# A decoder trunk's sparse layer: compressed scores right behind their keys, a new split of two weaves, and the last output tile in two pieces

## The chip, the cores and the metric

The kernel runs on one core of a Trainium2 chip. The core has five engines, each with its own stream of instructions: TensorE (PE; its weight loads are the row PEld), VectorE (DVE), ScalarE (ACT), GpSimd (POOL) and SyncE (SP), and 16 DMA engines. The metric is the time of one execution on the device in microseconds (us), of the whole program.

## What is computed

Two decoder layers over 256 tokens of width 1024, everything in f32. Layer 0 mixes with two sparse attentions side by side (MoBA and NSA, 8 heads each), layer 1 with differential attention; each is followed by a SwiGLU block of width 2816. Each sub-layer is normed, shifted and scaled by rows that come from a conditioning vector `c`, and its result is gated by such a row.

```python
def reference(x, c, ...):
    for i in range(DEPTH):
        mod = jax.nn.silu(c) @ ada_w[i] + ada_b[i]
        sh_a, sc_a, g_a, sh_f, sc_f, g_f = jnp.split(mod[:, None, :], 6, axis=-1)
        h = rms_norm(x, attn_norm[i]) * (1.0 + sc_a) + sh_a
        y = sparse_mixer(h, ...) if i % 2 == 0 else diff_mixer(h, ...)
        x = x + g_a * y
        h = rms_norm(x, ffn_norm[i]) * (1.0 + sc_f) + sh_f
        x = x + g_f * swiglu(h, ffn_w_gate[i], ffn_w_up[i], ffn_w_down[i])
    return x
```

The change lies in NSA's part of layer 0 and in the last lines of layer 1. NSA adds three attentions per head, each with its gate: over compressed keys and values, over selected blocks, over a window. With 256 tokens the last two cover all earlier tokens, each with its own keys. The compressed branch makes 15 keys and 15 values per group out of overlapping stretches of 32 tokens:

```python
def nsa_compress(t, pos_emb, w1, w2):
    blocks = t[:, :, idx] + pos_emb
    hid = jax.nn.silu(jnp.einsum('bgnld,lde->bgne', blocks, w1))
    return jnp.einsum('bgne,ed->bgnd', hid, w2)
...
        p_c = masked_softmax(jnp.einsum('bgrqd,bgnd->bgrqn', qg, kc) * scale, ok_c)
        o_c = jnp.einsum('bgrqn,bgnd->bgrqd', p_c.astype(vc.dtype), vc)
```

## The kernel before

**Precision and weights.** A large matmul is made of three (`mm3`, L250): both operands are split in a high and a low half, and high by high, high by low and low by high are added up in PSUM. `wunit` (L235) brings in one unit of weights: a load of 512 KB into one of five buffers `raw` (issued on SP, L240), then ScalarE writes the high half (`hi`, L188) and VectorE the low one (`lo`, L189). A `raw` buffer comes free with VectorE's half. The compression's weights (L1072) go through the same five `raw` buffers, but TensorE reads them there, so they come free with its matmuls. Loads of conditioning weights by `ada` (L276) have two buffers of their own (`araw`); those of `ada_pe` (L329) use `raw`.

**Order.** The program is written as generators, each of which yields after a piece of work. `weave` (L46) takes turns among several by weight: the generator whose count of turns divided by its weight is lowest goes next. The framework's scheduler then sets each engine's order out of that program and of its own estimates, so a change in the text at one place moves instructions on all engines nearby.

**Layer 0's sparse part.** A first weave (L1298) runs three generators. The first is `nsa_phase` (L975), followed by part of `nsa_heads` (L1152), weight 22; the second is `moba_proj` (L1175), the q, k and v projections of MoBA, weight 20; the third is `ada(0, 2)`, conditioning, weight 9. `nsa_phase` finishes NSA's queries and keys, then compresses keys (turn `v` = 0 of its loop) and values (`v` = 1): 16 products with the weights `w1` into a bank of the group CB (L1072 to L1076), a silu, a small product. For the keys the result is written to `kcT` (L1095). Only after both turns come the compressed scores (`kcT` by `qT` into a bank of CB), their softmax in `scc` (L1126 to L1140: VectorE, with one exp on ScalarE, L1133), two transposes on TensorE (L1144) and a copy to `pcT` (L1146). `nsa_heads` makes eight softmax steps, two for each pair of heads (two maps each, `softmax_maps` L878: scores, exp, then normalise and three transposes per map, L911, copied to `pT`, L913). After the second step of a pair it adds the compressed part (`vblk` by `pcT`). It yields three times per pair, and `first(nh, 6)` (L1280) lets six of its twelve turns run in the first weave: the four steps of the first two pairs.

A second weave (L1305) runs what is left of `nsa_heads`, then `moba_heads` (four steps), weight 22, against two `ada_pe` (conditioning products on TensorE, `raw` by `cs`), weight 14. Then comes the output projection. PSUM's eight banks are dealt out by group in `banks` (L89): in the first weave CB is bank 3 and TR (transposes) banks 6 and 7.

**The end.** The last SwiGLU block keeps its last three pairs of down-projection rows for two passes, one per half `t` of the tokens, each in two halves `f` of 512 columns (L679). `res_norm` (L442) then does, per half: multiply the bank by the gate row (L452), add to the residual (L455) and, at the very end, send it out (L457).

Of the kernel before, what the change touches and what calls it, by code (L numbers as in the profile page):

```python
# [17 lines left out]
P = 128  # L18
S = 256
# [45 lines left out]
def tile_trunk(ctx: ExitStack, tc: tile.TileContext, x, c, positions, ada_w, ada_b, attn_norm, ffn_norm,  # L65
# [36 lines left out]
    def tmp(shape, tag, bufs, dt=F32):  # L102
        return sp.tile(shape, dt, name=nm(tag), tag=tag, bufs=bufs)
# [338 lines left out]
    def res_norm(t, bs, g, i, js, hts):  # L442
# [117 lines left out]
    def ffn(i, hts, nxt, before_tail):  # L560
# [112 lines left out]
        for t in range(NT):  # L673
            keep = chain[:]
            chain[:] = tail
            for fs in ((0,), (1,)):
                for k in ks:
                    down_mm(t, k, us[k - ks[0]], fs)
            tail[:] = chain  # L679
            chain[:] = keep  # L680
            res_norm(t, BS, rows[(i, 5)], *nxt)
            yield
# [292 lines left out]
    def nsa_phase(hts):  # L975
# [72 lines left out]
        G.memset(kcT, 0.0)  # L1048
        vblk = tmp([P, 8, 64], "vblk", 1)
        for v in range(2):  # L1050
# [38 lines left out]
            if v == 0:  # L1089
# [26 lines left out]

        sc = tmp([P, NT, 4, 2, 16], "scc", 1)
        b = bank(*CB)
        for t in range(NT):
            for pr in range(4):  # L1120
                o = (t * 4 + pr) * 32
                mm(b[:, o:o + 32], lhsT=qT[:, pr, t * P:(t + 1) * P],
                   rhs=kcT[:, pr // 2].rearrange("p h n -> p (h n)"), start=True, stop=True)
        for t in range(NT):
            st = sc[:, t].rearrange("p a b n -> p (a b) n")
            V.tensor_tensor(out=st, in0=b[:, t * P:(t + 1) * P].rearrange("p (h n) -> p h n", n=16),  # L1126
                            in1=maskm[:, t:t + 1, :].broadcast_to([P, 8, 16]), op=ALU.add)
            V.tensor_tensor(out=st, in0=st, in1=nrs[:, t, :].unsqueeze(2).broadcast_to([P, 8, 16]), op=ALU.mult)
        s16 = sc.rearrange("p t a b n -> p (t a b) n")
        mx = tmp([P, 16], "cmx", 1)  # L1130
        V.tensor_reduce(out=mx, in_=s16, axis=AX.X, op=ALU.min)
        V.tensor_tensor(out=s16, in0=s16, in1=mx.unsqueeze(2).broadcast_to([P, 16, 16]), op=ALU.subtract)
        A.activation(out=s16, in_=s16, func=AF.Exp, scale=-1.0)  # L1133
        sm = tmp([P, 16], "csm", 1)
        V.tensor_reduce(out=sm, in_=s16, axis=AX.X, op=ALU.add)
        V.reciprocal(out=sm, in_=sm)
        V.tensor_tensor(out=sm.rearrange("p (t h) -> p t h", t=NT), in0=sm.rearrange("p (t h) -> p t h", t=NT),
                        in1=gts[:, :, 0:8], op=ALU.mult)
        V.tensor_tensor(out=s16, in0=s16, in1=sm.unsqueeze(2).broadcast_to([P, 16, 16]), op=ALU.mult)
        V.tensor_tensor(out=s16[:, 0:8, :], in0=s16[:, 0:8, :],  # L1140
                        in1=valid0.unsqueeze(1).broadcast_to([P, 8, 16]), op=ALU.mult)
        b = bank(*TR)
        for t in range(NT):
            T.transpose(out=b[:, t * P:(t + 1) * P], in_=sc[:, t].rearrange("p a b n -> p (a b n)"), identity=ident)  # L1144
        pcT = tmp([P, S], "pcT", 1)
        A.activation(out=pcT, in_=b[:, 0:S], func=AF.Copy)  # L1146
        yield
# [138 lines left out]
    def late(*gens):  # L1286
        for g in gens:
            yield from g
# [9 lines left out]
    weave((late(np_, first(nh, 6)), 22), (moba_proj(hts), 20), (ada(0, 2, pin=True), 9))  # L1298
# [6 lines left out]
    weave((late(nh, moba_heads(*om)), 22), (late(*[ada_pe(0, j, bank_tiles[3]) for j in (4, 3)]), 14))  # L1305
# [58 lines left out]
```

## Time and profile before

| | |
|---|---|
| time, median of three runs | 751.43 us (750.35 to 752.98) |
| the profiled execution | 752.87 us, of which the profile's span is 750.8 |
| mean granted clock of TensorE in it | 0.984 |
| PE, share of the span | 94% |
| DVE, ACT, POOL | 67%, 55%, 5% |
| DMA, bytes and mean rate | 159.41 MB, 212 GB/s |

The span is one execution as the profiler saw it; a row of a timeline gives the start in us from the span's start, the time from first start to last end of the records in it, the engine, the line, out<-in with the program's names, the shape, and how many records (x). In square brackets stands the idle time of that engine just before, and what ended it. Matmuls overlap, so the spacing of starts is what one costs. A matmul of plain f32 operands shows as two records, one of split halves as one. In rows of windows the granted clock of TensorE (PEclk) is a share of 2.4 GHz; 0.50 is 1.2 GHz.

### The profile page before, as it was taken

Reading aid. Unit: us, or ns where it says so; the run is one execution under the profiler, and the core shown is the slowest. Engines: PE = TensorE matmul, PEld = TensorE weight load, DVE = VectorE, ACT = ScalarE, POOL = GpSimd, SP = SyncE. Lnnn points to the kernel's source line nnn. Section 1 sums busy time; section 2 is a strip of 40 time slices with the busy share of each in tenths; the row PEclk is TensorE's granted clock in tenths of the full one; section 3 lists DMA queues with packets and bytes.
Section 4 is the critical chain, followed back from the end, with each engine's and each line's share of the span. In section 5 each row is a group of like instructions: output and inputs, shape, how many; then the busy total and the mean of one; then the engine's idle time right before and its main releaser. Section 6 shows DMA issues by size and latency. Waiting matters only on the chain.

```text
span 750.8 us, 10789 instructions
## 1 busy us (share of the span) xinstructions
PE 706.4 (94%) x3822; PEld 540.6 (72%) x3822; DVE 504.5 (67%) x1078; ACT 414.6 (55%) x813; POOL 40.8 (5%) x131
## 2 busy tenths in 40 slices
PE   5799899799989999999999999997989999999997
PEld 1368567445668878888887787763667888888885
DVE  3558565666587789788855765846777796655632
ACT  3465734688466456545544665566557465555530
POOL 5004102000000000000000021110000000000000
PEclk9999999799999999999999999899899999999999
DMA  9938286067538899998851564008937886566501
GB/s 321 379 127 313 76 296 246 1 234 276 192 91 274 284 339 338 314 305 299 280 193 60 196 223 141 29 18 304 345 113 257 309 292 212 172 196 192 179 20 57
DMA packets 86525, 159.41 MB, mean 212 GB/s; under 512 B 6199, under 2 KB 48316, under 8 KB 86472
## 3 DMA queue, kind: packets, MB, share of 16 engines
q1 hardware_dynamic: 85992, 158.72, 61.9%
q8 instruction: 30, 0.49, 0.3%
q14 instruction: 23, 0.19, 0.1%
q0 software_dynamic: 480, 0.01, 0.0%
HBM read 157.66 MB, written 1.05 MB: 211 GB/s over the span
## 4 chain that ended last, share of the span: by engine, by line
PE 77%; DMA 8%; DVE 6%; ACT 5%; issue 3%; SPq 1%; DVEq 0%; ACTq 0%
PE bank L116 73%; PE bank L911 2%; DMA araw<-in_ada_w_dram 2%; DMA bias<-in_ada_w_dram 2%; DMA raw<-in_ada_w_dram 1%; DMA raw<-in_sp_w_in_dram 1%; DVE lo L189 1%; DMA xs<-in_x_dram 1%; DMA raw<-in_ffn_w_gate_dram 1%; PE bank L711 1%; ACT hi L188 1%; DVE ada_acc L282 1%; PE bank L407 1%; ACT bigT L188 1%; DVE bigT L189 1%
## 5 line engine op out<-in xcount | busy, mean ns | idle before, releaser
L189 DVE TENSOR_TENSOR lo<-raw,hi 128x1024 fp32r<-128x1024 f32 x131 | 156.6, 1205 | 54.2 <-ACT hi L188 53.6
L188 ACT ACTIVATE hi<-raw 128x1024 fp32r<-128x1024 f32 x131 | 135.2, 1043 | 69.9 <-PE bank L116 43.3
L116 PE MATMUL bank<-hi,bigT 128*128 128x512 f32 (+1 forms) x472 | 154.0, 397 | 5.2 <-ACT bigT L188 4.4
L116 PE MATMUL bank<-bigT,hi 128*128 128x512 f32 (+1 forms) x400 | 130.8, 379 | 0.0
L116 PEld LDWEIGHTS bank<-hi,bigT 128*128 128x128 f32 x472 | 89.2, 192 | 26.0 <-ACT bigT L188 5.3
L116 PE MATMUL bank<-bigT,lo 128*128 128x256 f32 x368 | 98.5, 281 | 0.0
L116 PE MATMUL bank<-lo,bigT 128*128 128x512 f32 (+1 forms) x236 | 93.8, 398 | 0.5 <-DVE lo L189 0.4
L116 PEld LDWEIGHTS bank<-bigT,hi 128*128 128x128 f32 x400 | 71.7, 189 | 12.8 <-DVE lo L189 0.4
L282 DVE SCALAR_TENSOR_TENSOR ada_acc<-araw,cs,ada_acc 128x1024 f32<-128x1024 f32 x46 | 58.8, 1278 | 20.1 <-DMA araw<-in_ada_w_dram 20.1
L116 PEld LDWEIGHTS bank<-bigT,lo 128*128 128x128 f32 x368 | 69.5, 189 | 3.8 <-issue 0.2
L116 PEld LDWEIGHTS bank<-lo,bigT 128*128 128x128 f32 x236 | 45.3, 192 | 13.4 <-DVE lo L189 3.9
L892 DVE CUSTOM_DVE_ANT_0 s<-bank,maskc,nrs 128x128 f32<-128x128 f32 (+1 forms) x80 | 29.9, 412 | 32.0 <-PE bank L116 15.5
L620 ACT ACTIVATE w2k<-bank 128x256 f32<-128x256 f32 x64 | 23.9, 379 | 34.0 <-PE bank L116 34.0
L894 ACT ACTIVATE s<-s,mx 128x128 f32<-128x128 f32 (+1 forms) x80 | 35.7, 448 | 10.5 <-DVE mx L892 10.3
L621 DVE TENSOR_TENSOR w2k<-bank,w2k 128x256 f32<-128x256 f32 x64 | 26.5, 417 | 10.0 <-ACT w2k L620 10.0
L116 PE MATMUL bank<-bigT,nkv 128*128 128x256 f32 (+1 forms) x176 | 31.5, 322 | 0.0
L189 DVE TENSOR_TENSOR tok<-raw,tok 128x1024 fp32r<-128x1024 f32 x19 | 23.2, 1220 | 9.2 <-ACT tok L188 9.1
L188 ACT ACTIVATE nkv<-raw 128x1024 fp32r<-128x1024 f32 x19 | 20.1, 1057 | 16.1 <-PE bank L116 8.1
L189 DVE TENSOR_TENSOR nkv<-raw,nkv 128x1024 fp32r<-128x1024 f32 x19 | 23.2, 1222 | 7.7 <-ACT nkv L188 7.6
L188 ACT ACTIVATE tok<-raw 128x1024 fp32r<-128x1024 f32 x19 | 20.1, 1058 | 13.7 <-PE bank L116 9.5
L116 PEld LDWEIGHTS bank<-bigT,nkv 128*128 128x128 f32 x176 | 25.5, 188 | 2.8
L394 ACT ACTIVATE xn<-xs 128x512 f32<-128x512 f32 x16 | 10.1, 630 | 30.1 <-DVE xs L455 24.3
(342 smaller groups left out, 1257.7 us busy)
## 6 DMA issues: line engine op xcount, KB each, us to landing
araw<-in_ada_w_dram SPq DMA_DIRECT2D x50, 512.0 KB, 5.3
raw<-in_ffn_w_gate_dram SPq DMA_DIRECT2D x44, 512.0 KB, 5.1
raw<-in_ffn_w_up_dram SPq DMA_DIRECT2D x44, 512.0 KB, 4.9
raw<-in_ffn_w_down_dram SPq DMA_DIRECT2D x44, 512.0 KB, 5.2
raw<-in_ada_w_dram SPq DMA_DIRECT2D x32, 512.0 KB, 5.1
raw<-in_diff_w_in_dram SPq DMA_DIRECT2D x24, 512.0 KB, 4.5
raw<-in_sp_w_in_dram SPq DMA_DIRECT2D x20, 512.0 KB, 6.0
raw<-in_nsa_cmp_w_dram SPq DMA_DIRECT2D x8, 512.0 KB, 5.1
```

The lines of the kernel that those rows point to most:

```text
L116: ins = T.matmul(o, lhsT=lhsT, rhs=rhs, start=start, stop=stop).ins
L188: i1 = A.activation(out=hi, in_=src, func=AF.Copy)
L189: i2 = V.tensor_tensor(out=lo, in0=src, in1=hi.bitcast(F32), op=ALU.subtract)
L282: ins = V.scalar_tensor_tensor(out=acc, in0=raw, scalar=cs[:, k:k + 1], in1=acc, op0=ALU.mult, op1=ALU.add)
L394: return A.activation(out=junk[:, fs], in_=xs[:, t, fs], func=AF.Square, accum_out=ss[:, f:f + 1])
L407: q = T.transpose(out=b[:, k * P:(k + 1) * P], in_=xn[:, f * 512 + k * P:f * 512 + (k + 1) * P], identity=ident)
L620: A.activation(out=s[:, f * S:(f + 1) * S], in_=bs[f][:, S:512], func=AF.Copy)
L621: V.tensor_tensor(out=s[:, f * S:(f + 1) * S], in0=bs[f][:, 0:S], in1=s[:, f * S:(f + 1) * S], op=ALU.add)
L711: T.transpose(out=b[:, k * P:(k + 1) * P], in_=src[:, k * P:(k + 1) * P], identity=ident)
L892: V.tensor_tensor_reduce(out=s[:, o:o + n], in0=b[:, o:o + n], in1=maskc[:, S - n:S], scale=nr(t), scalar=3e38, op0=ALU.add, op1=ALU.min, ...
L894: A.activation(out=s[:, o:o + n], in_=s[:, o:o + n], func=AF.Exp, scale=-1.0, bias=mx[:, t:t + 1], accum_out=sm[:, t:t + 1])
L911: T.transpose(out=b[:, k * P:(k + 1) * P], in_=s[:, k * P:(k + 1) * P], identity=ident)
```

## The change

Three things. First, the block from the compressed scores to `pcT` becomes a function `compressed` and is called in turn `v` = 0, right after `kcT` is written; its scores go to a bank of TR instead of CB. Second, `first(nh, 6)` becomes `first(nh, 2)`, so two of the eight softmax steps of `nsa_heads` are left in the first weave; the weights of the first generators go from 22 to 18 and from 22 to 26. Third, the last quarter of the output (`t` = 1, `f` = 1 of layer 1) is made in two pieces of 256 columns: its 18 last matmuls become 36 of half the width, and multiply, add and output run once per piece.

```diff
@@ res_norm
+            if last and t and f:
+                for e in (512, 768):
+                    es = slice(e, e + 256)
+                    V.tensor_tensor(out=xn[:, es], in0=bs[t][f][:, e - 512:e - 256], in1=g[:, es], op=ALU.mult)
+                    V.tensor_tensor(out=xs[:, t, es], in0=xs[:, t, es], in1=xn[:, es], op=ALU.add)
+                    dma(out[0, t * P:(t + 1) * P, es], xs[:, t, es])
+                return
@@ ffn
+                if nxt[2] is None and t and fs[0]:
+                    for e in (0, 256):
+                        for k in ks:
...
+                            c = slice(512 + e, 768 + e)
+                            mm3(BS[t][1][:, e:e + 256], ah[:, cc], al[:, cc], hi[:, 0, c], lo[:, 0, c], False,
+                                e > 0 and k == ks[-1])
+                    continue
@@ nsa_phase
+        def compressed():
+            sc = tmp([P, NT, 4, 2, 16], "scc", 1)
+            b = bank(*TR)
...
+            pcT = tmp([P, S], "pcT", 1)
+            A.activation(out=pcT, in_=b[:, 0:S], func=AF.Copy)
+            return pcT
@@ nsa_phase, v == 0
                     A.activation(out=kcT[hs, :, half, 0:15], in_=bo[hs, 0:30].rearrange("p (g n) -> p g n", g=2),
                                  func=AF.Copy)
+                pcT = compressed()
@@ nsa_phase, behind the loop
-        sc = tmp([P, NT, 4, 2, 16], "scc", 1)
-        b = bank(*CB)
...
-        pcT = tmp([P, S], "pcT", 1)
-        A.activation(out=pcT, in_=b[:, 0:S], func=AF.Copy)
-        yield
         box.update(qT=qT, nrs=nrs, kT=kT, vv=vv, gts=gts, vblk=vblk, pcT=pcT)
@@
-    weave((late(np_, first(nh, 6)), 22), (moba_proj(hts), 20), (ada(0, 2, pin=True), 9))
+    weave((late(np_, first(nh, 2)), 18), (moba_proj(hts), 20), (ada(0, 2, pin=True), 9))
@@
-    weave((late(nh, moba_heads(*om)), 22), (late(*[ada_pe(0, j, bank_tiles[3]) for j in (4, 3)]), 14))
+    weave((late(nh, moba_heads(*om)), 26), (late(*[ada_pe(0, j, bank_tiles[3]) for j in (4, 3)]), 14))
```

The scheduler's orders differ in the two weaves, up to the start of the output projection, and at the end. Two places follow on SP and TensorE in the first weave, and one on VectorE at the end. A row is an instruction of one engine in its order, with the line (in the changed kernel lines stand 7 to 51 further down: L1072 is L1123, L1053 L1104, L711 L728, L911 L928; L1144 is L1095) and the engines that it waits for (DMAHW is a DMA).

**SP, loads in the first weave.** `in_nsa_cmp_w1` is the compression's weights, `in_sp_w_in` the projections', `in_ada_w` conditioning. Before, from the first load for the values on:

```order
L1072 DMA raw161_990<-in_nsa_cmp_w1_dram 128x4x256 [waits DMAHW5_49,DMAHW1_49,DVE_49]
L240 DMA raw162_996<-in_sp_w_in_dram 128x2x512 [waits PE_49]
L1072 DMA raw165_1014<-in_nsa_cmp_w1_dram 128x4x256 [waits DMAHW3_49,PE_49]
L276 DMA araw166_1020<-in_ada_w_dram 128x1024 [waits DMAHW4_49]
L240 DMA raw167_1023<-in_sp_w_in_dram 128x2x512 [waits DMAHW6_49,PE_49]
L1072 DMA raw170_1041<-in_nsa_cmp_w1_dram 128x4x256 [waits DMAHW7_49,PE_49]
L240 DMA raw171_1047<-in_sp_w_in_dram 128x2x512 [waits DMAHW2_49,DVE_49]
L1072 DMA raw174_1065<-in_nsa_cmp_w1_dram 128x4x256 [waits DMAHW5_49,DMAHW0_49,DVE_49]
L276 DMA araw175_1071<-in_ada_w_dram 128x1024 [waits DMAHW1_49]
L240 DMA raw180_1093<-in_sp_w_in_dram 128x2x512 [waits DMAHW7_49,DVE_49]
```

After:

```order
L240 DMA raw170_1044<-in_sp_w_in_dram 128x2x512 [waits PE_49]
L1123 DMA raw173_1062<-in_nsa_cmp_w1_dram 128x4x256 [waits DMAHW5_49,PE_49]
L240 DMA raw174_1068<-in_sp_w_in_dram 128x2x512 [waits DMAHW6_49,PE_49]
L240 DMA raw178_1089<-in_sp_w_in_dram 128x2x512 [waits DMAHW7_49,DMAHW4_49,DVE_49]
L1123 DMA raw181_1107<-in_nsa_cmp_w1_dram 128x4x256 [waits DMAHW0_49,PE_49]
L1123 DMA raw186_1123<-in_nsa_cmp_w1_dram 128x4x256 [waits DMAHW6_49,DVE_49]
L276 DMA araw177_1086<-in_ada_w_dram 128x1024 [waits DMAHW2_49,DVE_49]
L240 DMA raw198_1188<-in_sp_w_in_dram 128x2x512 [waits DMAHW7_49,DMAHW3_49,DVE_49]
...
L240 DMA raw212_1247<-in_sp_w_in_dram 128x2x512 [waits DMAHW3_49,DVE_49]
L240 DMA raw225_1307<-in_sp_w_in_dram 128x2x512 [waits DMAHW6_49,DVE_49]
L240 DMA raw228_1325<-in_sp_w_in_dram 128x2x512 [waits DMAHW7_49,DMAHW0_49,DVE_49]
```

The four loads for the values (the first, `raw169`, stands two rows ahead of these) are issued before the last four projection loads, and each projection load from `raw178` on waits for VectorE: for the low half of `raw170`, `raw178`, `raw198`, `raw212` and `raw225` in turn.

**TensorE, around the compressed scores** (`kcT` by `qT`) and the transposes of `scc`. Names: `hi` and `lo` are a unit's halves, `raw` by `od` a product of the compression, `bigT` the layer's input, `kTn` by `qT` a softmax step's scores. Before:

```order
L116 MATMUL bank_69<-hi_1414,bigT_105 128x512
L116 MATMUL bank_67<-kTn_772,qT_106 128x128
L116 MATMUL bank_70<-kcT_837,qT_106 128x32 [waits DVE_49]
L116 MATMUL bank_70<-kcT_837,qT_106 128x32 x7
L911 MATMUL bank_74<-ident,s_1234 128x128 [waits Activation_49]
...
L1144 MATMUL bank_73<-ident,scc_1111 128x128 [waits DVE_49]
L1144 MATMUL bank_73<-ident,scc_1111 128x128
```

After (`hi_1189` belongs to `raw198`, `hi_1248` to `raw212`, `hi_1308` to `raw225`):

```order
L116 MATMUL bank_68<-hi_1189,bigT_104 128x512 [waits Activation_49]
...
L116 MATMUL bank_73<-kcT_855,qT_106 128x32 [waits Activation_49]
L116 MATMUL bank_73<-kcT_855,qT_106 128x32 x7
L1104 MATMUL bank_73<-ident,nkv_108 128x128 [waits DVE_49]
L1104 MATMUL bank_73<-ident,nkv_109 128x128
L116 MATMUL bank_68<-hi_1248,bigT_104 128x512 [waits Activation_49]
L728 MATMUL bank_73<-ident,tok_1114 128x128 [waits Activation_49]
...
L116 MATMUL bank_70<-raw_1038,od_1033 30x256 [waits DMAHW2_49,DVE_49]
...
L1095 MATMUL bank_74<-ident,scc_978 128x128 [waits DVE_49]
...
L116 MATMUL bank_68<-hi_1308,bigT_105 128x512 [waits Activation_49]
```

The scores moved from behind the last projection matmul to between `hi_1189` and `hi_1248`; between them and the transposes of `scc` now stand 18 matmuls of 512 columns and most of the products for the values, which themselves moved behind the units `raw178`, `raw198` and `raw212`.

**VectorE, the last instructions.** Before:

```order
L452 TENSOR_TENSOR xn_6865<-bank_70,mod_6743 128x512 [waits PE_49]
L455 TENSOR_TENSOR xs<-xs,xn_6865 128x512 [waits DVE_49]
L1359 UNCONDITIONAL_BRANCH
```

After:

```order
L454 TENSOR_TENSOR xn_6883<-bank_70,mod_6743 128x256 [waits PE_49]
L454 TENSOR_TENSOR xn_6883<-bank_70,mod_6743 128x256
L455 TENSOR_TENSOR xs<-xs,xn_6883 128x256 [waits DVE_49] x2
```

Both multiplies stand ahead of both adds, and only the first waits for TensorE; `bank_70` is bank 3 in all four.

## Rows read from the trace of the kernel before

**Rows 1.** Page, part 1: busy time, share of the span, instructions of each engine.

```profile
PE 706.4 (94%) x3822; PEld 540.6 (72%) x3822; DVE 504.5 (67%) x1078; ACT 414.6 (55%) x813; POOL 40.8 (5%) x131
```

**Rows 2.** Windows: stretch, length, busy us of each engine, PEclk, DMA share.

```profile
80.00:84.00 4.00, 2.44 (x17) 1.31 (x15) 1.07 (x7) 2.83 (x10) 0.00 (x0) 1.00 0.01 2
106.00:120.00 14.00, 14.00 (x71) 9.14 (x69) 8.63 (x15) 7.90 (x12) 0.00 (x0) 1.00 0.93 338
132.00:136.00 4.00, 1.65 (x12) 0.77 (x11) 3.41 (x16) 1.96 (x7) 0.00 (x0) 1.00 0.02 4
136.00:140.00 4.00, 2.94 (x14) 1.94 (x14) 0.36 (x2) 2.23 (x6) 0.00 (x0) 0.56 0.00 0
140.00:144.00 4.00, 3.23 (x18) 2.24 (x15) 1.62 (x10) 1.98 (x7) 0.00 (x0) 0.50 0.00 0
144.00:148.00 4.00, 4.00 (x24) 2.46 (x20) 3.30 (x12) 2.87 (x10) 0.00 (x0) 0.66 0.00 0
466.00:470.00 4.00, 1.39 (x10) 0.92 (x8) 2.66 (x15) 3.62 (x12) 0.00 (x0) 1.00 0.00 0
470.00:474.00 4.00, 3.75 (x16) 2.61 (x17) 3.85 (x20) 2.92 (x12) 0.00 (x0) 0.62 0.01 4
```

**Rows 3.** Timeline, PE: start, us, line, operation, count, idle before.

```profile
128.30 1.97 PE L116 MATMUL bank<-kcT,qT 128*128 128x32 f32 x16
...
135.71 0.44 PE L1144 MATMUL bank<-ident,scc 128*128 128x128 f32 x2 [2.35 <-DVE scc L1140]
136.62 0.90 PE L911 MATMUL bank<-ident,s 128*128 128x128 f32 x3 [0.47 <-ACT pcT L1146]
138.10 1.12 PE L711 MATMUL bank<-ident,tok 128*128 128x128 f32 x4 [0.58 <-ACT pT L913]
...
142.94 1.12 PE L116 MATMUL bank<-pT,nkv 128*64 128x256 f32 x4 [0.77 <-ACT pT L913]
...
155.28 0.87 PE L911 MATMUL bank<-ident,s 128*128 128x128 f32 x6
...
198.19 0.86 PE L116 MATMUL bank<-pT,vm 128*64 128x256 f32 x6 [0.59 <-ACT pT L913]
```

**Rows 4.** Timeline, SP's queue, 101 to 113: issues of loads.

```profile
101.69 0.37 SPq L240 DMA_DIRECT2D raw<-in_sp_w_in_dram  x1
...
106.34 0.37 SPq L240 DMA_DIRECT2D raw<-in_sp_w_in_dram  x1
...
112.34 0.34 SPq L240 DMA_DIRECT2D raw<-in_sp_w_out_dram  x1
```

**Rows 5.** Timeline, ACT, same stretch: high halves of loads.

```profile
107.00 1.06 ACT L188 ACTIVATE hi<-raw 128x1024 fp32r<-128x1024 f32 x1 [4.45 <-DMA raw<-in_sp_w_in_dram]
110.00 1.06 ACT L188 ACTIVATE hi<-raw 128x1024 fp32r<-128x1024 f32 x1 [1.94 <-DMA raw<-in_sp_w_in_dram]
```

**Rows 6.** Timeline, DVE, same stretch: a low half.

```profile
111.08 1.23 DVE L189 TENSOR_TENSOR lo<-raw,hi 128x1024 fp32r<-128x1024 f32 x1 [1.77 <-ACT hi L188]
```

**Rows 7.** Timeline, PE, other places: durations and spacings.

```profile
104.40 7.09 PE L116 MATMUL bank<-raw,od 128*30 128x256 f32 x32
...
722.05 0.40 PE L116 MATMUL bank<-bigT,hi 128*128 128x256 f32 x2
...
722.41 0.40 PE L116 MATMUL bank<-bigT,hi 128*128 128x256 f32 x2
...
744.49 0.86 PE L116 MATMUL bank<-tok,kTm 128*128 128x512 f32 x3
745.19 0.85 PE L116 MATMUL bank<-nkv,kTm 128*128 128x512 f32 x3
```

**Rows 8.** Timeline, DVE, the end.

```profile
746.09 0.69 DVE L452 TENSOR_TENSOR xn<-bank,mod 128x512 f32<-128x512 f32 x1 [2.77 <-PE bank L116]
746.81 0.69 DVE L455 TENSOR_TENSOR xs<-xs,xn 128x512 f32<-128x512 f32 x1
```

**Rows 9.** Windows, the us after the last issue on SP.

```profile
748.00:749.00 1.00, 0.00 (x0) 0.00 (x0) 0.00 (x0) 0.00 (x0) 0.00 (x0) 1.00 0.64 244
```

More of the change, by code (lines that the diff above doesn't have):

```diff
@@ L1048, in nsa_phase @@
         G.memset(kcT, 0.0)
+        def compressed():
+            sc = tmp([P, NT, 4, 2, 16], "scc", 1)
+            b = bank(*TR)
+            for t in range(NT):
+                for pr in range(4):
+                    o = (t * 4 + pr) * 32
+                    mm(b[:, o:o + 32], lhsT=qT[:, pr, t * P:(t + 1) * P],
+                       rhs=kcT[:, pr // 2].rearrange("p h n -> p (h n)"), start=True, stop=True)
+            for t in range(NT):
+                st = sc[:, t].rearrange("p a b n -> p (a b) n")
+                V.tensor_tensor(out=st, in0=b[:, t * P:(t + 1) * P].rearrange("p (h n) -> p h n", n=16),
+                                in1=maskm[:, t:t + 1, :].broadcast_to([P, 8, 16]), op=ALU.add)
+                V.tensor_tensor(out=st, in0=st, in1=nrs[:, t, :].unsqueeze(2).broadcast_to([P, 8, 16]), op=ALU.mult)
+            s16 = sc.rearrange("p t a b n -> p (t a b) n")
+            mx = tmp([P, 16], "cmx", 1)
+            V.tensor_reduce(out=mx, in_=s16, axis=AX.X, op=ALU.min)
+            V.tensor_tensor(out=s16, in0=s16, in1=mx.unsqueeze(2).broadcast_to([P, 16, 16]), op=ALU.subtract)
+            A.activation(out=s16, in_=s16, func=AF.Exp, scale=-1.0)
+            sm = tmp([P, 16], "csm", 1)
+            V.tensor_reduce(out=sm, in_=s16, axis=AX.X, op=ALU.add)
+            V.reciprocal(out=sm, in_=sm)
+            V.tensor_tensor(out=sm.rearrange("p (t h) -> p t h", t=NT), in0=sm.rearrange("p (t h) -> p t h", t=NT),
+                            in1=gts[:, :, 0:8], op=ALU.mult)
+            V.tensor_tensor(out=s16, in0=s16, in1=sm.unsqueeze(2).broadcast_to([P, 16, 16]), op=ALU.mult)
+            V.tensor_tensor(out=s16[:, 0:8, :], in0=s16[:, 0:8, :],
+                            in1=valid0.unsqueeze(1).broadcast_to([P, 8, 16]), op=ALU.mult)
+            b = bank(*TR)
+            for t in range(NT):
+                T.transpose(out=b[:, t * P:(t + 1) * P], in_=sc[:, t].rearrange("p a b n -> p (a b n)"), identity=ident)
+            pcT = tmp([P, S], "pcT", 1)
+            A.activation(out=pcT, in_=b[:, 0:S], func=AF.Copy)
+            return pcT
         vblk = tmp([P, 8, 64], "vblk", 1)
@@ L1114, in nsa_phase @@
             yield
-        sc = tmp([P, NT, 4, 2, 16], "scc", 1)
-        b = bank(*CB)
[L1119 to L1144, printed above, removed]
-        pcT = tmp([P, S], "pcT", 1)
-        A.activation(out=pcT, in_=b[:, 0:S], func=AF.Copy)
-        yield
         box.update(qT=qT, nrs=nrs, kT=kT, vv=vv, gts=gts, vblk=vblk, pcT=pcT)
```

3 lines of the change are left out of this document (added).

## The prediction

> **What bounds the kernel now.** I read the busy shares first: TensorE is busy 706.4 of 750.8 us [rows 1], so only its idle time and its clock are to be had. Then the windows of the stretch that the change rewrites [rows 2]: while the projections of layer 0 run (106 to 120) TensorE has no gap with the DMA engines 0.93 busy; at 132 to 136 it is busy 1.65 of 4 us, and behind that its granted clock falls from 1.00 to 0.56, 0.50 and 0.66 (full speed is 2.4 GHz, 0.50 is 1.2). TensorE's own rows show why [rows 3]: the sixteen records of the compressed scores (128.30) come last of all, behind the last projection matmul, little is left to run beside their softmax, and the two transposes of `scc` wait 2.35 us on VectorE's last step of it; then three more small waits follow (0.47, 0.58, 0.77), since `pcT` and the maps' transposes are all that is left.
>
> So the place costs 4.17 us of idle time. The clock: from the means of the three windows it was low for 0.88 x 4 + 4 + 0.68 x 4 = 10.2 us, in which TensorE was busy about 8.5 (10.2 less the 0.58 and 0.77, and some of the 0.47); at full clock that work takes half, so 4.2 us are lost. Together 8.4 us.
>
> **Part 1, compressed softmax moved forward.** The same instructions run right behind the compressed keys, 8 scores and a chain of some 5.4 us on VectorE and ScalarE (128.30 + 1.97 to 135.71 [rows 3]). In the new order between the scores and the transposes of `scc` stand 18 matmuls of 512 columns and nearly all of the v products, over 10 us of TensorE's own work: the chain is covered. Gain: -8.4, all of it if nothing takes the hole's place.
>
> **Part 2, what the new order puts in its place.** The order on SP changes with it. `raw` has five buffers. Before, one load of the v-compress weights was issued at a time between projection loads. Now the four of them are issued early and hold four buffers until TensorE reaches the v products, which now stand behind most projections. So five projection loads (`raw178`, `raw198`, `raw212`, `raw225`, `raw228`) each wait on VectorE, that is for the split of the one before: one buffer, in series, from `raw170` on.
>
> One turn of that series: load issued to ScalarE's split, 3.66 us (106.34 [rows 4] to 110.00 [rows 5]); ScalarE to VectorE 1.08 (to 111.08 [rows 6]); VectorE's half 1.23; the next issue 0.03 later (112.34 [rows 4]). Sum 6.0. Four turns from the issue of `raw170` to the end of `raw212`'s split: 24.0.
>
> `raw170` is issued when TensorE has ended the first group of k products. From there to the low half of `raw212`, TensorE has: three groups of k products, 3 x 7.09/4 = 5.3; 49 matmuls of 512 columns at 0.233 (745.19 less 744.49, over three), 11.4 [rows 7]; the 8 scores, half of 1.97 [rows 3], since a matmul of f32 shows as two records, 1.0; 16 small transposes at 0.87/6, 2.3 [rows 3]. Sum 20.0. It waits 24.0 - 20.0 = **4.0 us**, most of it in one gap: from the low half of `raw198` it has 2.3 us of work until the high half of `raw212` comes, one load and one ScalarE split (4.7 us) later. The last two loads come while TensorE does the v products (7.1) and 17 matmuls, so they cost nothing; that cover gone, each would cost as much as that gap.
>
> The bounds of this term: nothing, if TensorE comes later to these rows than counted; and 7.3, if loads that share the DMA engines take what one with others in flight took, 101.69 to 107.00, 5.3 [rows 4, 5]; with that in two of the four turns the series takes 27.3. I take 3.66, since in a series fewer loads are in flight. What the row shows, 3.66 us, stands against the Trainium skill, "DMA: Bandwidth & Descriptors", section "Anatomy of one DMA — SWDGE (gpsimd) path": about 2.0 us fixed and the bytes at 436 GB/s. That gives an estimate of 3.2 us for 512 KB and a wait of 2.2 us in place of 4.0; the page's fit is for another issuing path, and the measurement decides.
>
> **Part 3, the clock in the new gap.** Before 136 TensorE waited 2.35 us and then 0.47, and the clock fell [rows 2, 3]; behind another stretch with gaps (466 to 470, busy 1.39 of 4) it fell as well, to 0.62 in the next four [rows 2]. The new gap before `raw212` is 4.7 - 2.3 = 2.4 us, then come one matmul and four transposes, then some 0.6 until its low half: the nearest row is the one that fell. So I count one fall as dear as the one removed: +4.2. Ends: 0, and 4.2 for a full one. The rule in "TensorE: Matmul & The Clock Gate" of the Trainium skill, section "HAM oscillation — how this bites in real kernels", is the same case: matmuls in groups that each wait for a load lose the clock between them; the trace agrees for a wait on VectorE, with 0.56 behind 132 to 136.
>
> **Part 4, weave.** Two of eight softmax steps instead of four now run beside the projections, so two go to the second weave, and its weights (26 against 14 instead of 22) let steps follow one another with less of the conditioning's matmuls between them. TensorE's work is the same. A step without filler waits for ScalarE's copy of a transposed map: 0.59 at full clock (198.19), 0.77 at half [rows 3]. I take one such wait, +0.6; the ends are 0 and six of them, 3.5, one for each of the six steps of `nsa_heads` then left.
>
> **Part 5, tail.** The last 18 matmuls of 512 columns become 36 of 256. Three of those take 0.36 (722.05 to 722.41 [rows 7]): 36 x 0.120 - 18 x 0.233 = +0.13. Both pieces lie in bank 3, and in the new order the first product waits once on TensorE and the second not at all: both come behind the last matmul, so VectorE's mult and add, 0.69 each [rows 8], stay behind TensorE. The last transfer is half as big; the DMA engines were busy 0.64 of the us after the old one's issue [rows 9], so some 0.3 is saved. Sum -0.1 to -0.2. If the pieces did overlap, one mult would hide: -0.7 more at most, the lower end. Against that overlap stands the Trainium skill, "PSUM — Partial Sum Buffer", section "PSUM bank collisions raise a hardware error": one engine may not read a bank's partitions while TensorE writes them. By that rule the pieces cannot overlap inside one bank, which is the sum as taken; no run here shows a collision.
>
> **Sum:** -8.4 + 4.0 + 4.2 + 0.6 - 0.1 = **+0.3**. The hole moves from behind the projections to between them. The durations come from an execution of 752.87 us, 1.44 above the median of 751.43; the median is the base, so 751.43 + 0.3 = **751.7**. A measurement of this kernel tells no more than about 0.3% (2.25 us) from no change.
>
> **Rivals.**
> - *The clock holds.* The gap is there, the fall is not. For: at 80 to 84 TensorE was idle 1.56 of 4 us and kept 1.00 [rows 2], and the work around the new gap is of full 512-column matmuls, not the thin ones of 128 to 136. Against: both longer gaps of the rows brought a fall. The sum without 4.2: 751.43 - 3.9 = 747.5.
> - *The loads come in time.* TensorE is behind its loads when the series begins, as it was before (14.00 of 14.00 busy at 106 to 120 [rows 2]), and the wait is filled. Then only 0.6 and -0.1 are left against -8.4: 743.5. Against: a turn of 6.0 us brings 12 matmuls, 2.8 us of work, and the v products that could fill it are placed behind.
> - *Slower: the series is longer.* The four v-compress loads and the conditioning's loads are in flight beside it, so that two of four turns cost 5.3 instead of 3.66; wait 7.3, the clock falls. 751.43 + 3.6 = 755.0. It decides once the series takes 2 us longer than 24.0. For: DMA engines 0.93 busy in that stretch before [rows 2]; against: part of those loads is then already in.
> - *It doesn't do what it says.* The chain of the compressed softmax is still late because `scc`'s VectorE steps queue behind the splits: hidden by 10 us, so small.
>
> **How the numbers follow.** Forecast (hole moved, clock falls) 0.34; clock holds 0.21; loads in time 0.17; longer series 0.23; not done as said 0.05. Faster by over 0.3% are the second and nearly all of the third: 0.37. Same are the forecast, the last and a little of the others: 0.38. Slower is most of the longer series and the forecast's upper end (six small waits): 0.25. The range leaves out the lowest part of "in time" and the highest of the last ones: 744.5 to 755.5; the forecast's own is 750 to 753.5.
>
> **What would show it.** Right: the stretch at 128 to 148 without the 2.35 us wait on VectorE; TensorE waiting on ScalarE's split of a load from in_sp_w_in, 3 us or more in all, between about 100 and 115, ScalarE itself waiting on the DMA; the clock at 0.5 to 0.7 some microseconds behind; projection loads on SP issued 6 us apart; the last product on VectorE right behind the last matmul. Wrong: no such wait (loads in time), or waits of 7 us and more (longer series), a clock at 1.00 through 100 to 150, or a new gap over 2 us in the second weave, which no term covers.

## The result, and the profile after

The change made the kernel slower: 756.04 us (median of 11 runs, 753.52 to 758.98) against 749.09 (11 runs, 746.88 to 753.23) for the kernel before on the same chip. The ratio is 1.0094, with a 95% interval of 1.0075 to 1.0113, so 7.0 us. The forecast was no change, +0.3; the time lies above the range, whose upper end was 755.5. (Ratios here and below are of fast runs alone; the medians given for `e5_mod2` and `g1_w1` hold one slow run each, 1156.99 and 976.11 us at a granted clock of 0.563 and 0.680, and are 753.81 and 754.36 without it.)

The two profiled executions differ by less than the medians, 753.52 (the lowest of its eleven) against 752.87: in the one of before TensorE reached the first transposes of `xn` at 44.36 us, in the one of after at 40.25, ahead of anything that the change touches, and two profiles of one and the same kernel show both values (40.5 in `f2_hid`, 44.6 in `h2_again`, below). So I compare stages. A stage begins at a row of transposes of `xn` (L407). The windows of TensorE by stage, first before, then after: stretch, length, busy us of PE, PEld, DVE, ACT and POOL (with counts), granted clock, DMA share, GB/s. The stages are layer 0's attention, layer 0's SwiGLU, layer 1's attention, and the rest.

```profile
44.36:210.84 166.48, 159.45 (x918) 108.48 (x919) 108.11 (x346) 102.39 (x258) 15.37 (x39) 0.97 0.56 193
210.84:408.72 197.88, 194.43 (x1022) 161.23 (x1021) 153.32 (x202) 107.51 (x160) 0.00 (x0) 1.00 0.77 261
408.72:553.15 144.43, 131.85 (x718) 98.76 (x716) 98.60 (x293) 89.91 (x218) 14.53 (x50) 0.95 0.51 175
553.15:750.80 197.65, 190.43 (x997) 160.13 (x995) 124.69 (x163) 96.55 (x142) 0.00 (x0) 1.00 0.55 181
```

```profile
40.25:214.30 174.05, 164.75 (x918) 111.93 (x919) 109.33 (x346) 103.55 (x258) 16.73 (x39) 0.95 0.56 187
214.30:411.00 196.70, 193.59 (x1019) 160.87 (x1018) 153.11 (x201) 107.67 (x160) 0.00 (x0) 1.00 0.78 262
411.00:554.00 143.00, 131.12 (x720) 98.39 (x719) 98.76 (x293) 90.10 (x217) 14.65 (x50) 0.96 0.51 177
554.00:751.00 197.00, 190.50 (x1016) 161.12 (x1014) 124.53 (x165) 96.67 (x142) 0.00 (x0) 1.00 0.56 182
```

In the second view the boundaries are rounded: the last three stages begin at 214.34, 411.69 and 554.10, so their lengths are 197.4, 142.4 and, to the span's end at 751.7, 197.6. The loss sits in the first stage: 7.6 us longer, with the same 918 matmul records. Idle time (length less busy) went from 7.0 to 9.3, busy time from 159.5 to 164.8. The last stage has not moved.

What stands now at the place of [rows 3], TensorE's timeline, and the windows that answer to [rows 2]:

```profile
106.75 0.79 PE L116 MATMUL bank<-hi,bigT 128*128 128x512 f32 x1 [3.48 <-ACT hi L188]
...
110.59 3.46 PE L116 MATMUL bank<-kcT,qT 128*128 128x32 f32 x16
114.70 0.69 PE L1104 MATMUL bank<-ident,nkv 128*128 128x128 f32 x2 [0.65 <-DVE scc L1077]
115.04 0.78 PE L116 MATMUL bank<-hi,bigT 128*128 128x512 f32 x1
116.61 1.12 PE L728 MATMUL bank<-ident,tok 128*128 128x128 f32 x4 [0.80 <-ACT w2k L1109]
...
129.38 0.44 PE L1095 MATMUL bank<-ident,scc 128*128 128x128 f32 x2
```

```profile
82.00:86.00 4.00, 3.35 (x9) 1.23 (x8) 3.88 (x13) 3.90 (x14) 0.00 (x0) 0.58 0.15 25
...
104.00:108.00 4.00, 1.25 (x4) 0.85 (x4) 3.04 (x10) 1.74 (x3) 0.00 (x0) 0.81 0.68 243
108.00:112.00 4.00, 4.00 (x16) 3.52 (x15) 0.16 (x1) 0.77 (x3) 0.00 (x0) 0.50 0.47 139
112.00:116.00 4.00, 3.16 (x13) 2.52 (x12) 1.85 (x5) 1.21 (x4) 0.00 (x0) 0.50 0.00 0
116.00:120.00 4.00, 3.39 (x10) 2.90 (x11) 4.00 (x10) 2.88 (x7) 0.77 (x1) 0.50 0.43 131
120.00:124.00 4.00, 4.00 (x18) 2.68 (x17) 3.73 (x7) 0.83 (x1) 3.51 (x7) 0.98 0.21 35
...
132.00:136.00 4.00, 4.00 (x23) 3.26 (x22) 0.00 (x0) 0.68 (x2) 0.00 (x0) 1.00 0.94 324
136.00:140.00 4.00, 4.00 (x16) 2.17 (x14) 0.02 (x1) 2.31 (x4) 0.00 (x0) 1.00 0.24 95
```

The old hole is gone: the transposes of `scc` (129.38) wait for nothing, and 132 to 140 is full at full clock. A larger one has opened: TensorE waits 3.48 us for ScalarE's high half of `raw198`, then 0.65 and 0.80, and its clock stays at 0.50 until 120. The two small waits are not for loads: the scores, the transposes of `nkv` and those of `tok` use one bank of TR in turn (`bank_73` in the order shown with the change), and each row of transposes waits until VectorE or ScalarE has emptied it. Why TensorE waits for `raw198`, from SP's queue, ScalarE and VectorE (the answers to [rows 4], [rows 5] and [rows 6]):

```profile
86.44 0.37 SPq L240 DMA_DIRECT2D raw<-in_sp_w_in_dram  x1
...
90.91 2.15 SPq L240 DMA_DIRECT2D raw<-in_sp_w_in_dram  x2
...
99.81 0.37 SPq L240 DMA_DIRECT2D raw<-in_sp_w_in_dram  x1
...
107.98 14.50 SPq L240 DMA_DIRECT2D raw<-in_sp_w_in_dram  x3
```

```profile
97.46 1.06 ACT L188 ACTIVATE hi<-raw 128x1024 fp32r<-128x1024 f32 x1 [1.95 <-DMA raw<-in_sp_w_in_dram]
...
105.64 1.06 ACT L188 ACTIVATE hi<-raw 128x1024 fp32r<-128x1024 f32 x1 [2.41 <-DMA raw<-in_sp_w_in_dram]
...
111.61 1.06 ACT L188 ACTIVATE hi<-raw 128x1024 fp32r<-128x1024 f32 x1 [2.64 <-DMA raw<-in_sp_w_in_dram]
```

```profile
114.15 0.49 DVE L1077 TENSOR_TENSOR scc<-bank,maskm 128x128 f32<-128x128 f32 x2 [5.99 <-PE bank L116]
...
114.96 1.22 DVE L189 TENSOR_TENSOR lo<-raw,hi 128x1024 fp32r<-128x1024 f32 x1
```

The load of `raw198` (issued at 99.81) took 5.83 us to its split, that of `raw212` (107.98) 3.63, and `raw212` was issued only once `raw198` was split: loads in series, as Part 2 said. `raw170` is the issue at 86.44, `raw178` the second of the two from 90.91; it was split at 97.46.

### The profile page after: what moved, and what is told of

It is laid out like the page before. It is cut to its first block, busy times and chain, and to the rows that moved or that the text cites. A ratio compares the mean times of both kernels' runs of the same rounds, so it can differ in the third digit from the quotient of the medians.

```text
span 751.7 us, 10826 instructions
## 1 busy us (share of the span) xinstructions
PE 705.6 (94%) x3840; PEld 542.9 (72%) x3840; DVE 505.1 (67%) x1080; ACT 416.4 (55%) x813; POOL 42.4 (6%) x131
## 4 chain that ended last, share of the span: by engine, by line
PE 78%; DMA 9%; ACT 5%; DVE 5%; issue 2%; SPq 1%; DVEq 0%
PE bank L116 75%; DMA raw<-in_sp_w_in_dram 3%; PE bank L928 2%; DMA bias<-in_ada_w_dram 1%; ACT hi L188 1%; DMA xs<-in_x_dram 1%; DMA araw<-in_ada_w_dram 1%; DMA raw<-in_diff_w_out_dram 1%; PE bank L728 1%; DVE lo L189 1%; DMA raw<-in_ffn_w_gate_dram 1%; DMA raw<-in_ada_w_dram 1%; PE bank L407 1%; ACT bigT L188 1%; DVE bigT L189 1%
## 5 line engine op out<-in xcount | busy, mean ns | idle before, releaser
L911 ACT ACTIVATE s<-s,mx 128x128 f32<-128x128 f32 (+1 forms) x80 | 35.8, 449 | 8.4 <-DVE mx L909 8.2
L188 ACT ACTIVATE tok<-raw 128x1024 fp32r<-128x1024 f32 x19 | 20.1, 1056 | 13.7 <-PE bank L116 13.0
L158 POOL TENSOR_SCALAR rs_w<-ss 128x16 f32<-128x16 f32 x7 | 3.3, 473 | 430.3 <-DVE ss L706 430.2
```

The costliest lines, as they stand in the source:

```text
L158: E.tensor_scalar(out=o, in0=i, scalar1=m, scalar2=c_, op0=ALU.mult, op1=ALU.add)
L188: i1 = A.activation(out=hi, in_=src, func=AF.Copy)
L911: A.activation(out=s[:, o:o + n], in_=s[:, o:o + n], func=AF.Exp, scale=-1.0, bias=mx[:, t:t + 1], accum_out=sm[:, t:t + 1])
```

## The experiments

Eleven runs of ten kernels, each beside the kernel before on the same chip.

**Parts alone.** `e1_tail`: the kernel before with the two edits of the tail alone (the first two pieces of the diff above).

> The kernel before with the third part alone: the last quarter of the output in two pieces. Loads theory (the loss is the projection loads in series in the first weave, with the clock fall behind their gap): this part is worth -0.1 to -0.2 us, ratio 1.000. Rival (the tail costs): up to +7 us. The trace should show both multiplies behind the last matmul. It also shows the first weave of the kernel before in a second execution, where the profiled one was 3.8 us above the median of the eleven runs.

Measured: 750.44 against 749.33, ratio 1.0016 (0.9991 to 1.0041). The tail is worth nothing that can be told. VectorE's last rows in the changed kernel (the answer to [rows 8]) say why:

```profile
747.04 0.76 DVE L454 TENSOR_TENSOR xn<-bank,mod 128x256 f32<-128x256 f32 x2 [2.79 <-PE bank L116]
747.71 0.75 DVE L455 TENSOR_TENSOR xs<-xs,xn 128x256 f32<-128x256 f32 x2
```

Both halves of the multiply stand behind the last matmuls, a row of three that starts at 746.48; nothing overlaps.

`e2_move`: the kernel before with `compressed` alone, weave numbers as before.

```diff
@@ nsa_phase, v == 0
+                pcT = compressed()
@@ nsa_phase, behind the loop
-        sc = tmp([P, NT, 4, 2, 16], "scc", 1)
...
```

> The kernel before with the first part alone: the compressed block right behind its keys, weaves as before (6 turns, 22 and 22). In its order the loads for the values alternate with the projection loads as before, and the transposes of scc have about 30 matmuls ahead of them. Loads theory: no gap at the loads, the hole at 132 to 146 and its half clock go: -5 to -8.4 us, ratio 0.989 to 0.993. Rival (moving the block itself is harmful, its scores in a transposes' bank and its steps ahead of the splits on VectorE): no gain or a loss, ratio 1.00 or more, with waits at the transposes of the values' input.

Measured: 752.89, ratio 1.0043 (1.0014 to 1.0072), so the gain that was expected did not come. The hole is gone here too, but the loads come late in two places (waits of 1.36 us at 105.59 and 1.62 at 111.63 on ScalarE's split), and the values' products stand later (115.93, in the kernel before 104.40). In its profile the stage is 172.9 us, 6.5 longer than before's, and that is more than the waits: TensorE is busy 164.7 us in it, in the kernel before 159.5, at the same mean clock of 0.97. So the move alone also makes the same records cost more; the rows on `kTn` below show where a part goes. By the medians it loses a little, not 7 us.

`e3_weave`: the weave numbers alone.

```diff
-    weave((late(np_, first(nh, 6)), 22), (moba_proj(hts), 20), (ada(0, 2, pin=True), 9))
+    weave((late(np_, first(nh, 2)), 18), (moba_proj(hts), 20), (ada(0, 2, pin=True), 9))
...
-    weave((late(nh, moba_heads(*om)), 22), (late(*[ada_pe(0, j, bank_tiles[3]) for j in (4, 3)]), 14))
+    weave((late(nh, moba_heads(*om)), 26), (late(*[ada_pe(0, j, bank_tiles[3]) for j in (4, 3)]), 14))
```

> The kernel before with the second part alone: first(nh, 2) and weights 18 and 26, the compressed block where it was. Its order on SP has the same series of projection loads as the change. Loads theory: a gap of 3 to 4 us at a load with the clock fall behind it, and the old hole as well: +6 to +14 us, ratio 1.008 to 1.019. Rival (the move of the block makes the loss): ratio 1.000, within 2 us.

Measured: 756.96, ratio 1.0099 (1.0063 to 1.0135), as slow as the whole change. It has the new gap (2.33 us on ScalarE's split, at 105.95) and keeps the old hole (1.66 on `scc`, at 138.51).

`g1_w1` and `g2_w2`: the first and the second of those two lines, each alone.

> The kernel before with the first weave's numbers alone (first(nh, 2) and 18); second weave 22, block and end as before. Loads theory: the series of projection loads comes from these numbers, so the loss of the weaves is here, ratio 1.007 to 1.014. Rival (the second weave's 26 makes it): ratio 0.998 to 1.003.

> The kernel before with the second weave's weight alone (26 for 22). Loads theory: 0 to +1 us, ratio 0.999 to 1.002, a few more short waits of TensorE for copies of maps. Rival (the second weave carries the loss): ratio 1.006 or more.

Measured: `g1_w1` 754.59, ratio 1.0073 (1.005 to 1.0096); `g2_w2` 750.06, 1.0012 (0.9989 to 1.0035). The loss is the first weave's: with fewer softmax steps between projections and compression, TensorE runs out of its units there. In `g1_w1` the gap is 3.87 us, yet the clock comes back sooner. Windows of `g1_w1`:

```profile
104.00:108.00 4.00, 1.17 (x5) 0.86 (x5) 1.95 (x6) 1.74 (x3) 0.00 (x0) 0.91 0.61 210
108.00:112.00 4.00, 4.00 (x20) 3.54 (x19) 3.52 (x8) 3.23 (x10) 0.79 (x1) 0.66 0.46 131
112.00:116.00 4.00, 4.00 (x19) 2.20 (x19) 1.56 (x2) 1.34 (x2) 3.17 (x11) 1.00 0.11 9
```

What follows the gap differs with the length of the fall (one profile of each; no run changed that work alone): in the changed kernel there are the sixteen thin records of the scores and two more waits (busy 3.16 and 3.39 of 4 us at 0.50), in `g1_w1` there is no idle time at all.

**The series of loads.** `e5_mod2`: the changed kernel, with the first two loads of the values in the idle buffers `mod` in place of `raw`.

```diff
-                raw = raw_tile().rearrange("p (k n) -> p k n", k=4)
+                raw = (tmp([P, 1024], "mod", 2) if v and u < 2 else raw_tile()).rearrange("p (k n) -> p k n", k=4)
```

> The change, with two of the four loads for the values put into the two buffers mod, which are idle until the end of the first weave, so that raw has two more buffers for projection loads. Nothing is left out. Loads theory: projection loads no longer wait for the split of the one before; the gap at about 103 to 107 and the clock fall go, and the change's own gain shows: 11 to 15 us below the change, 741 to 745 us where before is 749. Rival (the loss comes from the second weave or the compressed block's own waits): within 3 us of the change.

Measured: 754.06, ratio 1.0073 (1.0045 to 1.0101). The cure took: beside the projections TensorE's longest wait is 0.89 us, at 106.83 (later 1.25, at 193.69, on a copy of a map), and the clock doesn't fall in the stage:

```profile
40.31:207.22 166.91, 159.53 (x918) 107.62 (x919) 109.05 (x346) 102.49 (x258) 16.57 (x39) 1.00 0.60 195
```

That is 7 us shorter than the changed kernel's stage, but no shorter than the kernel before's, whose hole is gone here: TensorE is busy 159.5 us at full clock, where the kernel before had 159.5 with 4.4 lost to the clock, so its own work costs 4.5 more. And the median is only 2 us better than the change's, which by its number is the rival's case: layer 1's attention, which has no edit, is 147.0 against 142.4. The series is not the whole of the loss, and both points come back in the next runs.

**The block behind the values.** `f1_behind` calls `compressed` right behind the sixteen products of the values, `f2_hid` behind their hidden layer; weave numbers and tail as before. So the loads of the values keep their old place and the chain still has projections beside it.

```diff
@@ nsa_phase, behind the sixteen products
+            if v:
+                pcT = compressed()
```

> Weaves as before (6 turns, 22 and 22), no change at the end, the compressed block called in turn v = 1, right behind the sixteen products for the values, so that it does not stand ahead of them. Its order keeps the loads of the kernel before, with the values' products where they were, and has the transposes of scc some 20 matmuls ahead of the end of the projections. Loads theory (what costs in the change is that the values' products, and with them four raw buffers, are put off): the hole at 132 to 146 goes and nothing takes its place, 3 to 8 us faster than before, ratio 0.989 to 0.996. Rival (TensorE pays the hole back as other waits or as slower sequences of its own matmuls wherever the block stands): ratio 0.997 to 1.004.

> As the run before, with the block called a step later, behind the values' hidden layer, so that its transposes come behind the last projection loads but still ahead of the last projection matmuls. Loads theory: like it, 3 to 8 us faster than before, with at most a short wait at the transposes. Rival: ratio 0.997 to 1.004.

Measured: `f1_behind` 748.71 against 749.14, ratio 0.9994 (0.9966 to 1.0023); `f2_hid` 747.24, 0.997 (0.9949 to 0.9991). Windows of `f2_hid`, layer 0's attention and layer 1's:

```profile
40.50:201.70 161.20, 158.41 (x918) 107.99 (x919) 109.13 (x346) 103.54 (x258) 17.39 (x39) 1.00 0.60 201
398.11:548.02 149.91, 134.20 (x718) 99.96 (x717) 99.25 (x293) 89.88 (x218) 14.41 (x50) 0.94 0.50 169
```

Layer 0 gains 5.3 us (idle 2.8, clock 1.00). Layer 1 loses 5.5, though no line of it differs: the scheduler's estimates shifted with the edit, and it put six products of `vm` by `pT` in another place. TensorE's timeline in `f2_hid`:

```profile
463.18 1.24 PE L116 MATMUL bank<-kTn,qT 64*128 64x128 f32 x8
464.34 0.94 PE L116 MATMUL bank<-vm,pT 128*128 128x128 f32 x6
468.49 0.94 PE L116 MATMUL bank<-vm,pT 128*128 128x128 f32 x6 [3.22 <-ACT od L1271]
```

All twelve records stand behind the scores, the last six wait for a copy that ScalarE does behind its exps; in the kernel before six stand ahead of those scores (at 473.43) and the others follow without a wait.

To test that cause I looked for small changes of the first weave's weights that leave TensorE's order in layer 1's attention as it was. `h1_order` is `f2_hid` with the weight 22 at 20; `h2_again` is `f2_hid` unchanged; `i2_ada7` is `f1_behind` with the conditioning's weight 9 at 7.

```diff
-    weave((late(np_, first(nh, 6)), 22), (moba_proj(hts), 20), (ada(0, 2, pin=True), 9))
+    weave((late(np_, first(nh, 6)), 22), (moba_proj(hts), 20), (ada(0, 2, pin=True), 7))
```

> The compressed block behind the values' hidden layer, as in the run f2_hid, with the first weave's weight at 20 instead of 22. In layer 1 this gives TensorE the order of the kernel before again: the six products of `vm` by `pT` stand three ahead and three behind a head's scores, where f2_hid had all six behind them and TensorE waited 3.22 us on ScalarE's copies. Theory (that order is what gave the gain back): no wait over 2 us at 450 to 480, layer 1 as long as in the kernel before (144.4 us from its first transposes to those behind its output projection, f2_hid 149.9), median 742 to 745. Rival (layer 1 is longer whenever layer 0 ends early, since its loads and its clock don't come earlier): layer 1 stays at 148 to 150, median 746 to 749. A third: the weight of 20 itself opens a gap at the projections, as 18 did, and layer 0 is longer by 3 us or more than in f2_hid.

> The kernel of f2_hid once more, beside h1_order on the same chip. If its 0.997 was no accident: 0.995 to 0.999, median some 2 us below the kernel before, with the wait of 3.2 us on ScalarE near 468 in the profile again. If it was: 1.000 to 1.003.

> The compressed block right behind the sixteen products of the values, as in the run f1_behind, the first weave's weights 22 and 20 as in the kernel before, and only the conditioning's weight there at 7 instead of 9. In layer 1 TensorE has the order of the kernel before again (six products of `vm` by `pT`, three ahead and three behind a head's scores). Theory (the wait on ScalarE behind that order in layer 1 gave back the gain of layer 0): no wait over 2 us near 460 to 480, layer 1 at 143 to 146 us between its first transposes and those behind its output projection (f1_behind 148.0, f2_hid 149.9, h1_order 143.4); and, with no gap in the projections, layer 0's sparse part at 161 to 163; then the median is 742 to 745, below h1_order's 747.6. Rival (layer 1 takes back what layer 0 saves in any order): layer 1 at 148 or more, median 746 to 749. Third: the weight of 7 moves loads and opens a gap of over 1 us at 100 to 120; then layer 0's part is 164 or more and the median 746 to 748.

Measured: `h1_order` 747.58 against 748.98, ratio 0.998 (0.9955 to 1.0006); `h2_again` 746.96, 0.9993 (0.9966 to 1.0021); `i2_ada7` 745.97 against 749.21, 0.9969 (0.9948 to 0.999). So `f2_hid` is at best a little faster than the kernel before. In `h2_again` layer 1's attention is 150.6 us again; in both others the wait of 3.2 us is gone and it is 143.4 and 141.4. In `h2_again` the wait itself is 1.78 us, not the 3.2 expected, with the clock at half for 13.7 us around it. Over all profiles layer 1's attention is 147.0 to 150.6 us in the four that wait there (`e5_mod2` and `f1_behind` 1.66 each) and 141.4 to 146.3 in the others. So the theory holds for layer 1. In layer 0 neither did what it was made for: `h1_order` has a gap of 2.44 us on ScalarE's split at 104.69 (the third case of its expectation; stage 166.1 us), and `i2_ada7` has none, and still its stage is as long as before's, which no case had said:

```profile
40.72:207.56 166.84, 163.19 (x918) 109.52 (x919) 109.08 (x346) 104.22 (x258) 15.47 (x39) 1.00 0.58 194
403.99:545.40 141.41, 130.06 (x718) 97.54 (x717) 98.53 (x293) 90.28 (x218) 14.59 (x50) 0.98 0.53 179
```

With 918 records TensorE is busy 163.19 us at full clock, against 158.41 in `f2_hid`. Rows of one operation show where part of such differences goes. TensorE's scores in the kernel before, then in the changed one, then in `i2_ada7`:

```profile
148.60 0.93 PE L116 MATMUL bank<-kTn,qT 64*128 64x128 f32 x8
```

```profile
139.24 0.70 PE L116 MATMUL bank<-kTn,qT 64*128 64x256 f32 x2
...
141.99 1.32 PE L116 MATMUL bank<-kTn,qT 64*128 64x128 f32 x8
```

```profile
120.34 0.92 PE L116 MATMUL bank<-kTn,qT 64*128 64x128 f32 x4
```

A score matmul of one head contracts over 64 rows, half of the array, and a pair of heads lies on the two halves. Eight records take 0.93 us where the order alternates between two heads, and the starts then come in pairs some 10 ns apart (160.25 and 160.26 in the kernel before, there `kTn` with `kTm`); 1.32 where the starts come singly, one head and then the other; and four take 0.92 where one head stands alone. So a head that stands alone costs twice. TensorE's busy time on the tile `kTn`, 90 to 215 us, before, after and in `e2_move` (stretch, length, busy, clock, DMA share, GB/s):

```profile
90.00:215.00 125.00, 8.07 (x52) 0.96 0.57 200
```

```profile
90.00:215.00 125.00, 9.65 (x52) 0.95 0.57 189
```

```profile
90.00:215.00 125.00, 11.08 (x52) 0.97 0.57 194
```

The same 52 records cost 1.58 us more after the change and 3.0 more in `e2_move`, at full clock in all three. No kernel changed the pairing alone, so it is not shown how much of TensorE's extra work is due to it, and the pairing doesn't decide by itself: from 78 to 215 us `f2_hid`, the kernel with the shortest stage, spends 12.82 on `kTn`, more than the changed kernel's 12.17. Of the 4.8 us between `f2_hid` and `i2_ada7`, `kTn` has 0.9 (12.82 and 13.74), the conditioning's products with `cs` 1.4 (9.89 and 11.28), those with `pT` 1.2 (16.94 and 18.12).

## Why the prediction was wrong

It had the mechanism: the hole moves in between the projections, TensorE waits there for ScalarE's split of a load that came in series, and the clock falls behind it. It failed in the length of the series (Part 2), in the price of the fall (Part 3) and in "TensorE's work is the same" (Part 4), all to the same side. Terms of layer 0's attention, in us:

| term | forecast | measured |
|---|---|---|
| old hole (Part 1) | -8.4 | gone: idle -4.2, clock -4.4 |
| series of loads (Part 2) | +4.0 | +4.9 (3.48 for a load, 0.65 + 0.80 for a bank) |
| clock behind it (Part 3) | +4.2 | +6.0, and +1.5 at 82 to 86 |
| second weave's waits (Part 4) | +0.6 | +1.6 |
| TensorE's own work (Part 4) | 0 | +2.2 |
| sum | +0.4 | +7.6 |

The clock's entries are busy time below full speed, record by record, times what the granted clock lacks to 1; TensorE's own work is what is left of its busy time.

*Part 1 right.* The chain is covered by projections and the values' products; in `e2_move` projections alone cover it (scores at 99.31, transposes of `scc` at 109.56, without a wait).

*Part 2 is the first step that failed: the turn.* A turn was priced at 6.0 us, four of them at 24.0. They took 6.25, 7.1, 8.2 and 8.2, together 29.7 (`raw170` issued at 86.44, `raw178` at 92.7, `raw198` at 99.81, `raw212` at 107.98, its low half done at 116.18). Two turns were long by their loads, 4.8 and 5.83 from issue to split where 3.66 was taken: together the two of 5.3 that the rival "the series is longer" had counted. The fourth had a fast load, 3.63, but VectorE stood in the first step of `scc`, waiting for the scores until 114.15, and reached the low half at 114.96, though the high half was done at 112.67; no term held that. The gap came one load earlier than forecast, before `raw198`, whose load was the slowest, and not before `raw212`. That the waits, 4.9, lie so near the 4.0 is in part luck. Only 3.48 is a wait for a load; 0.65 and 0.80 come from the moved scores' bank of TR, as said above, which I had left out; and the half clock made TensorE's own work longer, which filled the rest of the series. The count of that work had a slip besides: eight scores are all of the sixteen records, 1.97 us, not half of them, so the work was 21.0 and the term, as priced, 3.0. The Trainium skill, "DMA: Bandwidth & Descriptors", section "Anatomy of one DMA — SWDGE (gpsimd) path", had given 3.2 us: the measured loads of 3.63, 4.8 and 5.83 are all longer.

*Part 3 is the second step that failed, by size.* "I count one fall as dear as the one removed": by the means of the windows from 104 to 124 the clock was at half for 0.38 x 4 + 12 + 0.04 x 4 = 13.7 us, with 1.25 + 4.00 + 3.16 + 3.39 + 0.16 = 12.0 us of busy time in it, so 6.0 lost. The nearest row was the right one in kind; it could not tell how long this fall would be. The prediction had counted "one matmul and four transposes, then some 0.6" behind the gap; as the gap came one load earlier, the thin scores and two waits on their bank follow it. `g1_w1` shows the other end, a gap of 3.87 us with full work behind it. That this work sets the length of the fall is likely by the two, and not shown. The second fall, at 82 to 86, lies behind waits that the kernel before has too (it kept 1.00 there [rows 2]); e2_move, e3_weave and h1_order show it, others don't, so I don't put it down to the change.

*Part 4 is the third step that failed.* "TensorE's work is the same": the instructions are, their time is not. Busy time rose by 5.3 us; 3.1 of it is the clock (7.5 less 4.4), 2.2 is work at full clock. The pairs of scores that came apart account for 1.6, by the rows above. TensorE's waits from 140 us on came to 2.2 (0.49, 1.23 and 0.47) against 0.6 in the kernel before (the old hole aside), so 1.6 more where 0.6 was counted: the largest is on ScalarE's copy of a map, at 200.84. Weight 26 has no part in it (g2_w2).

*Part 5 right:* nothing.

The rival nearest in time was "the series is longer", 755.0, and its condition came true: it was to decide once the series takes 2 us longer than 24.0, and it took 5.7 longer, by two slow loads as it said and by VectorE. But its sign, waits of 7 us and more, did not come. The waits were 4.9, and the rest of the loss is the clock and TensorE's own work, so it is in part luck that its number lies near. "The clock holds" and "the loads come in time" fell; and where the loads did come in time, in `e5_mod2`, the time was 754.06 and not the 743.5 of that rival, since TensorE's own work took 4.5 more and layer 1 lost 2.6. The named signs came out: waits on ScalarE's split of 3 us and more near 105, ScalarE itself on the DMA, issues on SP 8.2 us apart (99.81 to 107.98) where 6 were said. What the signs did not include is the length of the half clock and any change of TensorE's busy time on the same work, and there the loss lay.

Profiles differ from the medians by what the change doesn't touch: without the first 40 us (44 in the kernel before), the profiled execution of after is 5.0 longer than that of before, layer 1 giving back 2.0. With the same order in layer 1, e1_tail and g2_w2 show 143.6 and 145.1 there, so this is within what one profile tells.

## What to carry to other kernels

When a block is moved forward, ask which buffers the work that it displaces holds meanwhile: here four of five load buffers waited for products that the new order had put behind the loads. Count a turn of such a series by its slowest load and by every engine that has a hand in it: here 24.0 us became 29.7. Price a stall together with the work behind it: 3.48 us of waiting with thin work behind had the clock down four times as long as 3.87 us with full work. And where a scheduler writes the order, compare it on every engine over the whole program, also for pairs that run together only as neighbours: an edit in layer 0 lost 5.5 us in layer 1, and `i2_ada7`, the block behind the values with that order kept, came out faster than both kernels (0.9969 of the kernel before, measured once; `f2_hid`'s 0.997 was 0.9993 when measured again; the change is at 1.0094).

## What the runs showed of the hardware that was not expected

- Two 64-row matmuls on different halves of the array ran at the same time where they were neighbours in the order, and not otherwise: 8 records in 0.93 us alternating, 1.32 head by head, 4 in 0.92 alone. The Trainium skill, "TensorEngine Tiling (Array Packing)", section "Restrictions and Gotchas", says that such row tiles go to different banks; in the program each head's scores have a bank of their own, so the fast rows do alternate between two, but the trace doesn't name banks and no run put two heads into one.
- Behind a gap of 3.48 us the clock was at half for 13.7 us; behind one of 3.87, with TensorE full afterwards, for 0.18 x 4 + 0.68 x 4 = 3.4 us (the windows of g1_w1 from 104 to 112). "TensorE: Matmul & The Clock Gate" of the Trainium skill, section "HAM oscillation — how this bites in real kernels", describes such a fall in groups that wait for loads; the trace agrees, with 0.50 from 108 to 120.
- With the same waits before it (1.07 and 0.64 us in g1_w1, 1.06 and 0.64 in e3_weave), the clock fell near 83 us in `e3_weave` and not in `g1_w1`: some 1.7 us that no order explains.
